# Gaps of 96 bytes between the chunks of a weight block's high and low parts

## The chip, the core and the metric

The kernel runs on one core of a Trainium2 chip. The metric is the device time of one execution in microseconds. Three timed runs of the kernel before took 2360.72, 2362.53 and 2367.87 us; the median, 2362.53, is what the change is held against.

## What is computed

Two transformer stacks, one after the other, on one sequence of 256 tokens of width 1024, all in float32. The first has two layers with three kinds of attention heads and a gated MLP; the second has two layers that mix 256 latent and 256 context tokens through a gated recurrence, a differential attention and a Fourier branch. Cut to the part that the change touches, every layer is a chain of products with large weights:

```python
for l in range(DEPTH):
    h = _rms(x, ln1[l]) * (1 + sc1) + sh1
    x = x + g1 * _mixing(h, w_in[l], ..., w_o[l], cos, sin)
    h = _rms(x, ln2[l]) * (1 + sc2) + sh2
    x = x + g2 * _swiglu(h, w_gate[l], w_up[l], w_down[l])
...
aq, ak, av, ag, ao, az, bq, bk, bv, bz, cu, cz, mg = split_cols(h @ w_in)
y = g_a * (y_a @ w_a_out) + g_b * (y_b @ w_b_out) + g_c * (y_c @ w_c_out)
return y @ w_out
```

## The kernel before

**Blocks and parts.** A weight matrix is read in blocks of up to 8 chunks; a chunk is 128 rows of the matrix, one on each partition, and mostly 256 columns. `fetch` (L356) issues the loads of a block into the tile `raw`. `split_half` (L383) then makes two tiles of it, half a block at a time: `whi`, a copy rounded to the type `float32r`, on ScalarE, and `wlo`, the rest `raw - whi`, on VectorE, or for a few blocks on POOL. There are two buffers of each, `whi0` and `whi1`, `wlo0` and `wlo1`, used in turn.

**Products.** The activations are kept as a high and a low part too: `h` (two tiles `h2`, of which the context tokens have the first half of each chunk and the latent ones the second), `ahi` and `alo` in the MLP, `part`, `fhi` and `yacc` later on. `mm3` (L505) makes a product out of three matmuls for each chunk k: high with high, high with low, low with high. All matmuls of a product add into one place in PSUM.

```python
        for k in order or range(kch):
            for i, j in ((0, 0), (0, 1), (1, 0)):
                self.nc.tensor.matmul(ps, lhsT=lsl(lhs[i], k), rhs=rsl(rhs[j], k), ...)
```

`lhsT` is the operand that is loaded into TensorE's array, 128 columns of it; `rhs` is the one that streams. Two helpers call `mm3`. In `dense_t` (L517) the weight block is loaded and the activation streams, 256 or 512 columns; a profile row shows it as `ps_..<-h,whi`. In `dense_n` (L523) the activation is loaded and the 256 columns of the block stream: `ps_mm<-whi,h`. So each product with a full block is 24 matmuls in a row, and blocks follow each other without a pause where nothing is late. The MLP and the merges at the end of a layer are made with `dense_t`, most of the projections with `dense_n`.

**Order.** The program is written out ahead of time by a planner (`Clock`, `Pipe`) that estimates when each engine is free. It reads the shapes of operands and which ranges of a tile an instruction touches.

**Places.** All tiles of a block keep their place for the whole program. A chunk of a full block takes 1024 bytes of a partition, and chunk k of `whi` or `wlo` begins k times 1024 bytes behind the tile's first byte. As the program lays its tiles out, `whi0`, `whi1`, `wlo0` and `wlo1` all begin at 160 modulo 512, and so does each of their chunks. The chunks of `h`, `part`, `fhi` and `yacc` all begin at 480 modulo 512, those of `ahi` and `alo` at 288 in the first layer and 384 in the second. One kind of block is narrow, the 16 gate columns of the second stack (`a_gates`): its chunks are 64 bytes wide and so stand at eight places modulo 512 already.

Of the kernel before, what the change touches and what calls it, by code (L numbers as in the profile page):

```python
# [8 lines left out]
F32R = mybir.dt.float32r  # L9
# [11 lines left out]
DEPTH = 2  # L21
KC = D // 128
WB = 256
D_FF = 2816
FC = D_FF // 128
EPS = 1e-6
# [277 lines left out]
class Program:  # L304
# [51 lines left out]
    def fetch(self, j, now):  # L356
        kch, pieces = self.order[j]
        if j >= 2 and j - 2 >= self.ns or (not now and self.wp.free("raw", 2) > self.clock.t["pe"] + self.p.AHD):
            return False
        t = self.wp.tile([128, KC * WB], F32, name="raw", bufs=2)  # L360
        n = sum(p[4] for p in pieces)
# [19 lines left out]
    def split_half(self, now=True):  # L381


        j = self.ns
        if j >= self.nd or (j >= 2 and j - 2 not in self.consumed):
            return False
        if not now and self.clock.ready([self.blk[j][0]]) > self.clock.t["pe"] + 1:
            return False
        raw = self.blk[j][0]
        kch, pieces = self.order[j]  # L390
        n = sum(p[4] for p in pieces)
        if self.half == 0:
            for i, nm in ((1, "whi"), (2, "wlo")):
                t = self.wp.tile([128, KC * WB], F32R, name=f"{nm}{j % 2}")
                self.blk[j][i] = t[:, :kch * n].rearrange("p (k c) -> p k c", k=kch)
        k0, k1 = ((0, (kch + 1) // 2), ((kch + 1) // 2, kch))[self.half]
        hi, lo = self.blk[j][1], self.blk[j][2]
        if k1 > k0:
            self.nc.scalar.copy(hi[:, k0:k1], raw[:, k0:k1])
            e = self.nc.gpsimd if str(self.half) in self.p.SPOOL and self.every else self.nc.vector  # L400
            e.tensor_tensor(lo[:, k0:k1], raw[:, k0:k1], hi[:, k0:k1].bitcast(F32), op=ALU.subtract)
        self.half += 1
        if self.half == 2:
            self.half = 0
            self.ns += 1
        return True
# [1667 lines left out]
```

## Time and profile before

| | |
|---|---|
| median of three runs | 2362.53 us |
| the profiled execution | 2364.57 us |
| its span, first to last instruction | 2362.8 us |
| TensorE, matmuls | 2247.8 us busy, 95% |
| TensorE, weight loads | 1974.9 us, 84% |
| VectorE | 1287.4 us, 54% |
| ScalarE | 1032.1 us, 44% |
| POOL | 371.7 us, 16% |
| mean granted clock of TensorE | 0.969 |

The busy time of an engine is the time in which at least one of its instructions runs. Matmuls are pipelined: the next begins before the last has ended, so their durations add up to more than the busy time, and the pace of a row of matmuls is read from their starts. All instructions that helpers issue have one line, L170, in this program; groups are told apart by the names of their tiles, output first, then the operands, for a matmul the streaming one before the loaded one.

### The profile page before, as it was taken

The page shows a single profiled execution, that of the slowest core. Times are in us where ns is not written, and L with a number is a line of the kernel's source. Part 1 is how long each engine was busy: PE and PEld are TensorE (multiplying, and loading weights), DVE is VectorE, ACT ScalarE, POOL GpSimd, SP SyncE. Part 2 cuts the span into 40 slices and gives each one's busy share as a digit, 9 for nine tenths or more (in the row PEclk, how much of TensorE's full clock was granted, in tenths as well). Part 3 has the DMA queues.
Part 4 walks back from the last instruction along what each step waited for, and adds up shares of the span by engine and source line. Part 5 has one row for each costly group of instructions (what it writes and reads, how often), then busy time and mean ns, then how long its engine had stood idle before and what let it go on. Part 6 is the DMA issues. An engine that isn't in the chain of part 4 may idle for free. (4 is left out here: it accounts for less than half of the span.)

```text
span 2362.8 us, 39015 instructions
## 1 busy us (share of the span) xinstructions
PE 2247.8 (95%) x15672; PEld 1974.9 (84%) x15672; DVE 1287.4 (54%) x2547; ACT 1032.1 (44%) x1994; POOL 371.7 (16%) x897
## 2 busy tenths in 40 slices
PE   7989999998899999997989999999999999989999
PEld 3756899876899988887878888888898897989999
DVE  3735556575556546666554424335364656655665
ACT  3543445445444444554543323223254445444543
POOL 3311001551000103122022000000020333220000
PEclk8978999998999999998999999999999999999999
DMA  9646985655686522122114434434343232337865
GB/s 331 230 159 220 288 252 181 212 188 196 197 243 187 173 89 72 56 82 72 61 65 139 128 91 113 119 94 114 96 131 90 81 99 74 106 114 201 211 172 170
DMA packets 395061, 348.52 MB, mean 148 GB/s; under 512 B 12768, under 2 KB 364384, under 8 KB 394368
## 3 DMA queue, kind: packets, MB, share of 16 engines
q1 hardware_dynamic: 386752, 321.29, 45.1%
q0 software_dynamic: 6688, 21.66, 2.9%
q10 hardware_dynamic: 1440, 3.08, 0.4%
q8 instruction: 123, 2.02, 0.4%
q14 instruction: 58, 0.48, 0.1%
HBM read 335.50 MB, written 10.49 MB: 146 GB/s over the span
## 5 line engine op out<-in xcount | busy, mean ns | idle before, releaser
L170 DVE TENSOR_TENSOR wlo<-raw,whi 128x1024 fp32r<-128x1024 f32 (+1 forms) x465 | 547.6, 1210 | 449.1 <-ACT whi L170 447.8
L170 ACT CAST whi<-raw 128x1024 fp32r<-128x1024 f32 (+3 forms) x476 | 471.5, 1031 | 216.1 <-PE ps_t L170 63.3
L170 PE MATMUL ps_mm<-whi,h 128*128 128x256 f32 x2752 | 533.9, 291 | 16.1 <-ACT whi L170 6.2
L170 PEld LDWEIGHTS ps_mm<-whi,h 128*128 128x128 f32 x2752 | 440.6, 194 | 48.7 <-issue 19.3
L170 PE MATMUL ps_mm<-wlo,h 128*128 128x256 f32 x1376 | 391.1, 284 | 7.5 <-DVE wlo L170 7.3
L170 PE MATMUL ps_mm<-h,whi 128*128 128x256 f32 (+2 forms) x1656 | 375.5, 321 | 1.9 <-DVE xT L170 1.8
L170 PEld LDWEIGHTS ps_mm<-h,whi 128*128 128x128 f32 (+1 forms) x1656 | 269.2, 187 | 46.9 <-issue 9.0
L170 PEld LDWEIGHTS ps_mm<-wlo,h 128*128 128x128 f32 x1376 | 266.8, 194 | 12.6 <-DVE wlo L170 8.4
L170 PE MATMUL ps_mm<-h,wlo 128*128 128x256 f32 (+2 forms) x828 | 263.0, 318 | 1.1 <-POOL wlo L170 1.1
L170 PE MATMUL ps_s<-h,whi 128*128 128x256 f32 (+1 forms) x1120 | 240.2, 310 | 0.0
L170 PE MATMUL ps_t<-h,whi 128*128 128x256 f32 (+1 forms) x1096 | 234.9, 310 | 2.1 <-ACT h L170 1.5
L170 PEld LDWEIGHTS ps_s<-h,whi 128*128 128x128 f32 x1120 | 181.3, 188 | 18.3 <-ACT th L170 5.6
L170 PEld LDWEIGHTS ps_t<-h,whi 128*128 128x128 f32 x1096 | 179.0, 190 | 19.8 <-ACT th L170 6.3
L170 PE MATMUL ps_s<-h,wlo 128*128 128x256 f32 (+1 forms) x560 | 173.4, 310 | 0.1
L170 PE MATMUL ps_t<-h,wlo 128*128 128x256 f32 (+1 forms) x548 | 169.5, 309 | 0.0
L170 PEld LDWEIGHTS ps_mm<-h,wlo 128*128 128x128 f32 (+1 forms) x828 | 155.1, 187 | 14.7 <-POOL wlo L170 1.3
L170 PE MATMUL ps_g<-gw,c 128*32 128x512 f32 (+1 forms) x640 | 100.8, 640 | 18.0 <-DMA gw<-in_w_mod_dram 8.7
L170 PEld LDWEIGHTS ps_s<-h,wlo 128*128 128x128 f32 x560 | 105.2, 188 | 7.0 <-DVE wlo L170 0.3
L170 PEld LDWEIGHTS ps_t<-h,wlo 128*128 128x128 f32 x548 | 104.2, 190 | 6.2 <-DVE wlo L170 0.2
L170 ACT ACTIVATE M<-ps_s,nmB,rsB 128x512 f32<-128x512 f32 (+1 forms) x96 | 67.0, 702 | 94.2 <-DVE nmB L170 94.2
L170 DVE SCALAR_TENSOR_TENSOR y<-th,y 128x512 f32<-128x512 f32 (+1 forms) x64 | 35.6, 556 | 81.2 <-ACT th L170 67.9
L170 POOL TENSOR_TENSOR sqa<-sqa,sq 128x256 f32<-128x256 f32 x30 | 22.1, 736 | 346.9 <-ACT sq L170 191.3
(406 smaller groups left out, 3726.8 us busy)
## 6 DMA issues: line engine op xcount, KB each, us to landing
raw<-in_w_in_dram SPq DMA_DIRECT2D x72, 1024.0 KB, 5.3
raw<-in_w_in_dram SPq DMA_DIRECT2D x100, 512.0 KB, 4.1
gw<-in_w_mod_dram SPq DMA_DIRECT2D x96, 512.0 KB, 5.3
gw<-in_w_ada_dram SPq DMA_DIRECT2D x64, 384.0 KB, 5.0
raw<-in_w_gate_dram SPq DMA_DIRECT2D x44, 512.0 KB, 4.1
raw<-in_w_up_dram SPq DMA_DIRECT2D x44, 512.0 KB, 5.6
raw<-in_w_down_dram SPq DMA_DIRECT2D x16, 1024.0 KB, 5.1
raw<-in_w_out_dram SPq DMA_DIRECT2D x12, 1024.0 KB, 5.2
```

Source lines behind the costliest of these rows:

```text
L170: return real(*a, **k)
```

## The change

A constant `WPAD` of 24 elements, 96 bytes, is added. The tiles `whi` and `wlo` become 8 times 96 bytes larger, and the view of a block in them leaves 96 bytes free behind each chunk. `raw`, the loads and the matmuls stay as they are; the copies and subtractions write (and the subtraction reads back) four rows of 256 elements with gaps instead of one row of 1024.

```diff
+WPAD = 24
...
         if self.half == 0:
             for i, nm in ((1, "whi"), (2, "wlo")):
-                t = self.wp.tile([128, KC * WB], F32R, name=f"{nm}{j % 2}")
-                self.blk[j][i] = t[:, :kch * n].rearrange("p (k c) -> p k c", k=kch)
+                t = self.wp.tile([128, KC * (WB + WPAD)], F32R, name=f"{nm}{j % 2}")
+                self.blk[j][i] = t[:, :kch * (n + WPAD)].rearrange("p (k c) -> p k c", k=kch)[:, :, :n]
```

A chunk of a full block now begins 1120 bytes behind the one before it, which is 96 modulo 512: the eight chunks of `whi` begin at 160, 256, 352, 448, 32, 128, 224 and 320 modulo 512. Each of the four tiles takes 8960 bytes instead of 8192, so that `wlo0` and `wlo1` begin at 416 modulo 512 and `whi1` at 160 as before. The order of instructions on all engines is the same, row for row; only the shapes of the copies and subtractions differ.

## Rows read from the trace of the kernel before

**Rows 1.** The page: busy time by engine, and the granted clock in 40 slices.

```profile
PE 2247.8 (95%) x15672; PEld 1974.9 (84%) x15672; DVE 1287.4 (54%) x2547; ACT 1032.1 (44%) x1994; POOL 371.7 (16%) x897
...
PEclk8978999998999999998999999999999999999999
```

**Rows 2.** Waits of PE: us in total, times, longest us.

```profile
PE ps_mm L170 <- DVE wlo L170: 7.3, 5, 2.1
PE ps_mm L170 <- ACT whi L170: 6.2, 3, 3.0
```

**Rows 3.** Groups of PE by form: xcount | busy us, mean ns | idle before.

```profile
L170 PE MATMUL ps_mm<-whi,h 128*128 128x256 f32 x2752 | 533.9, 291 | 16.1 <-ACT whi L170 6.2 <-ACT h L170 5.5 <-DVE pq L170 2.1
L170 PE MATMUL ps_mm<-wlo,h 128*128 128x256 f32 x1376 | 391.1, 284 | 7.5 <-DVE wlo L170 7.3 <-POOL wlo L170 0.2
L170 PE MATMUL ps_mm<-h,whi 128*128 128x256 f32 x1112 | 203.9, 284 | 1.9 <-DVE xT L170 1.8
L170 PE MATMUL ps_mm<-h,whi 128*128 128x512 f32 x512 | 161.6, 397 | 0.0
```

**Rows 4.** Timeline of PE, 1870.2 to 1872.9: start us, us from first start to last end.

```profile
1870.03 0.28 PE L170 MATMUL ps_mm<-wlo,h 128*128 128x256 f32 x1
...
1870.50 0.39 PE L170 MATMUL ps_mm<-whi,h 128*128 128x256 f32 x2
...
1871.18 0.39 PE L170 MATMUL ps_mm<-whi,h 128*128 128x256 f32 x2
...
1871.52 0.39 PE L170 MATMUL ps_mm<-whi,h 128*128 128x256 f32 x2
```

**Rows 5.** Timeline of PE, 1893.6 to 1896.3, first and last of an even pace.

```profile
1893.81 0.28 PE L170 MATMUL ps_mm<-wlo,h 128*128 128x256 f32 x1
...
1895.93 0.28 PE L170 MATMUL ps_mm<-wlo,h 128*128 128x256 f32 x1
```

**Rows 6.** Stretches: window, us, then busy us of each engine, PEclk, DMA share.

```profile
2141.20:2299.20 158.00, 158.00 (x1343) 157.97 (x1342) 96.78 (x136) 74.83 (x112) 4.29 (x8) 1.00 0.73 194
2300.00:2359.00 59.00, 59.00 (x523) 59.00 (x522) 36.98 (x53) 24.93 (x35) 0.00 (x0) 1.00 0.61 177
1300.00:1700.00 400.00, 400.00 (x1749) 328.19 (x1748) 160.61 (x184) 117.63 (x150) 8.59 (x16) 1.00 0.40 109
```

**Rows 7.** Timeline of PE, 1500.0 to 1501.4, 512 columns.

```profile
1500.42 0.39 PE L170 MATMUL ps_t<-part,wlo 128*128 128x512 f32 x1
1500.64 0.62 PE L170 MATMUL ps_t<-part,whi 128*128 128x512 f32 x2
```

**Rows 8.** Timeline of PE, 836.4 to 839.6, the block of 16 columns.

```profile
836.93 0.62 PE L170 MATMUL ps_mm<-h,whi 128*16 128x512 f32 x2
...
839.02 0.62 PE L170 MATMUL ps_mm<-h,whi 128*16 128x512 f32 x2
```

**Rows 9.** Timeline of PE, 404 to 405.3, the MLP's last product.

```profile
403.79 0.28 PE L170 MATMUL ps_t<-ahi,whi 128*128 128x256 f32 x1
...
405.22 0.28 PE L170 MATMUL ps_t<-ahi,whi 128*128 128x256 f32 x1
```

**Rows 10.** Timeline of PE, 1803.8 to 1805.5, 512 columns at another pace.

```profile
1804.34 0.63 PE L170 MATMUL ps_mm<-h,whi 128*128 128x512 f32 x2
...
1805.04 0.63 PE L170 MATMUL ps_mm<-h,whi 128*128 128x512 f32 x2
```

**Rows 11.** Groups of ACT and DVE by form: xcount | busy us, mean ns | idle before.

```profile
L170 ACT CAST whi<-raw 128x1024 fp32r<-128x1024 f32 x452 | 455.4, 1048 | 203.0 <-PE ps_mm L170 60.0 <-PE ps_t L170 57.5 <-PE ps_s L170 53.0
...
L170 ACT CAST whi<-raw 128x768 fp32r<-128x768 f32 x16 | 12.5, 832 | 13.1 <-PE ps_t L170 5.8 <-PE ps_s L170 4.9 <-PE ps_mm L170 2.4
...
L170 ACT ACTIVATE eB<-eB 128x768 f32<-128x768 f32 x8 | 6.5, 841 | 0.2
...
L170 DVE TENSOR_TENSOR wlo<-raw,whi 128x1024 fp32r<-128x1024 f32 x441 | 529.0, 1232 | 426.2 <-ACT whi L170 425.0 <-PE ps_mm L170 0.5
...
L170 DVE TENSOR_TENSOR oB<-oB,roB 128x1024 f32<-128x1024 f32 x4 | 4.9, 1223 | 6.0 <-POOL roB L170 6.0
```

## The prediction

> **What bounds the kernel now.** I read the page's busy shares first [rows 1]: TensorE is busy for 2247.8 of 2362.8 us (95%), and the granted clock is nine tenths or more in nearly every slice; VectorE stands at 54%, ScalarE at 44%. Next come the waits of TensorE [rows 2]: the longest entry on a weight block is 7.3 us for `wlo` and 6.2 us for `whi`, eight waits in all. So the splits that the change reshapes are hidden, and what counts is how fast one matmul follows another.
>
> Then the groups by form give the numbers of matmuls [rows 3]. The change touches the two operands of every one that reads a weight block: 4,128 that stream 256 columns of `whi` or `wlo` (2752 + 1376), about 6,400 that stream 256 columns of an activation over weights loaded from `whi` or `wlo`, and about 2,250 of the second kind with 512 columns. That is nearly all of TensorE's time.
>
> The pace is read from starts in the timeline, since durations overlap. The reader should see that identical matmuls with 256 columns run at two paces. In [rows 4] a group of 24 begins unevenly (from 1870.03 to 1870.50 are four, 118 ns each) and then settles at 0.34 us for three, 113.3 ns each. In [rows 5] a group of the same form stays at 117.8 ns: from 1893.81 to 1895.93 are eighteen, in 2.12 us. Long stretches say the same [rows 6]: 158.0 us hold 1343 matmuls, the next 59.0 us 523. One or two of each count reach over the edges, which makes 117.8 and 113.3 ns, for the same kind of matmul at the same granted clock of 1.00, the 2.4 GHz level. With 512 columns 400.0 us hold 1749 (229 ns). A pace, once found, is kept: nothing in the other engines' columns goes with it.
>
> Counted over all starts inside unbroken runs of equal matmuls (the first and last of them being rows like those), the mean is 115.4 ns where the weight block streams (3,632 intervals, about half at each pace), 117.05 where it is loaded (5,907, mostly the slow pace) and 229.1 with 512 columns (2,213).
>
> **What the change does to this.** Before, each of a block's chunks begins at 160 modulo 512 and each chunk of `h` at 480, so that every matmul of a run meets its weight load in the same relation, and a steady pace can form. Afterwards the relation moves by 96 bytes at every chunk, that is every three matmuls, and `wlo` starts 256 away from `whi` besides. My reading is that no pace can settle, and that TensorE works on as it does where it has not settled.
>
> The trace has that state. At the start of runs the first three intervals have a mean of 117.3 ns where the block streams (134 runs), 117.4 where it is loaded (65 runs) and 231.7 with 512 columns (23 runs), before the settled means above. Two other rows agree. The block of 16 columns already stands at eight places modulo 512, its chunks being 64 bytes apart: from 836.93 to 839.02 nine matmuls take 232.2 ns each [rows 8]. And where `ahi` and `alo` stream, at 288 modulo 512 instead of 480, twelve take 119.2 ns each, from 403.79 to 405.22, and keep neither pace [rows 9]. Against it: the 16 columns are a short load, and `ahi` keeps one relation throughout, so neither is the changed state itself.
>
> **The sum**, against the profiled execution's 2364.57 us (span 2362.8):
> - block streams: 3,632 x (117.3 - 115.4) = +6.9 us;
> - block is loaded, 256 columns: 5,907 x (117.4 - 117.05) = +2.1 us;
> - 512 columns: 2,213 x (231.7 - 229.1) = +5.8 us.
>
> That is +14.8 us of TensorE, of which 95% (its busy share) reaches the end: +14.1. The matmuls outside unbroken runs are set by what they wait for and are taken at nothing. 2364.57 is 2.0 above the median of the three runs, so 2362.5 + 14.1 gives 2376.6, in round numbers **2377 us**.
>
> The cost of an unsettled pace lies between bounds. Below: every run finds the fast pace, 113.3 ns, and the 512-column ones the 226 ns that is the shortest of the three intervals that repeat there (1500.42 to 1500.64 in [rows 7]; the other two are 229 and 232). That is 3,632 x 2.1 + 5,907 x 3.75 + 2,213 x 3.1 = 36.6 us, down to 2326. Above: 118.8 ns, the mean with `ahi` and `alo` over 296 intervals, and 233.3, at which one group with 512 columns already stands: from 1804.34 to 1805.04 are three [rows 10]. That is 12.3 + 10.3 + 9.3 = 32 us, up to 2394. I take the start-of-run value, which is nearest to a relation that keeps changing, and keep both ends for the range.
>
> **The other edits.** The casts and subtractions write four rows of 256 with a gap instead of 1024 in one piece. ScalarE shows rows with a gap: `eB`, two rows of 384, takes 841 ns where the flat cast of 768 takes 832 [rows 11], so 9 ns for one gap and some 27 for three; I allow twice that, 54. 452 casts give 24 us of ScalarE's time at the most, under TensorE's. VectorE's `oB`, also in rows, takes 1223 ns for 1024 where the flat subtraction takes 1232: nothing. POOL, busy for 16% [rows 1], does 11 of the subtractions; no row of it has gaps at that size, and if they took half as long again, the block that they belong to would still be needed later. If the cover fails, the eight waits for a block grow by 0.05 us each: 0.4 us. A split that got faster would gain no more than those waits, 13.5 us. The low and high tiles grow by 768 bytes each; what stands after them moves by 3072 bytes, six times 512, so nothing else changes place modulo 512. The order of all instructions, DMAs and loads is the same row for row; no queue is passed and no wait added.
>
> **A rule against this.** The rows show paces that differ by 4.5 ns with nothing else changed. The Trainium skill, TensorE: Matmul & The Clock Gate, section Step-by-step: what each phase is for, says that TensorE reads the streamed operand and the weights through two independent ports, so that a load takes nothing from the running matmul; its section Back-to-back issue gap puts the gap at N / 2.4 + 2.5 ns, an estimate of 109.2 and 215.8 ns here. The trace disagrees with the figures: no settled pace is below 113.3 and 229. By that rule the places don't matter and the time stays at 2362.5.
>
> **The rivals.**
> 1. *It makes no difference* (0.19). What sets the pace is the rhythm of starts, not bytes. For it: two paces at equal addresses [rows 6], and the 16-column block, whose intervals don't follow its moving place [rows 8]. Against it: the pace with `ahi` is neither of the two [rows 9]. Then the gaps alone are left and hidden: 2362.5, within 3 us. That the change doesn't take effect at all belongs here; the tiles are laid out anew for every block, so I don't expect it.
> 2. *It is faster* (0.25). The mechanism: loads and streams that begin at the same place hold each other up at each start, and this is the slow pace; at eight places most chunks miss each other, and a run that misses once falls into 113.3 and stays, as in [rows 4]. The place is the loaded blocks, 5,907 intervals now mostly at 117.8. It decides the sign when three in ten runs come to the fast pace: 0.3 x 36.6 us is then as much as 0.7 x 14.8. All of them give 2326, half of the saving 2344. Against it: the fast pace also needs a steady relation, as far as any row shows.
> 3. *It is slower by more* (in my 0.56): every chunk meets a relation like that of [rows 9], 2394.
>
> **How the numbers follow.** About 0.3% (7 us) is what a measurement of this kernel can tell from no change. The forecast case has 0.56; some 0.05 of it ends below 2369.6 and counts as the same. With rival 1 that makes 0.24 the same; rival 2 is faster, 0.25; slower is left with 0.51. The range reaches to 2396 for rival 3 and down to 2336, seven tenths of rival 2's saving, and leaves out the ends of both. The forecast case alone runs from 2364 to 2396.
>
> **What would show it.** In the changed profile: if right, the timeline of a group of 24 has no settled 0.34 or 0.35 us for three, 158 us of the last stretch hold about 1,340 matmuls again, the stretch of 59 us fewer than 523, and 400 us of 512-column work about 1,727 instead of 1,749. Right for the splits: `whi` up to 1.10 us, waits of TensorE for blocks near 13 us. If the last stretch moves to 1,390 or more in 158 us, rival 2 holds; if both paces are found again with sharp steps between runs, rival 1. I would be wrong in the size if the unsettled mean is not 117 but near one of the ends, and in the mechanism if a pace settles in spite of the moving places.

## The result and the profile after

The changed kernel takes 2377.66 us (median of five runs, 2374.23 to 2382.75) where the kernel before takes 2360.72 (five runs, 2353.09 to 2367.87): a ratio of 1.0072, with a 95% interval of 1.0051 to 1.0094. That is 17 us slower. The profiled execution after is the one of 2377.66 us, its span 2375.9, its mean granted clock 0.978 (before 0.969).

The page's busy line and granted clock answer to [rows 1]:

```profile
PE 2256.8 (95%) x15672; PEld 1978.3 (83%) x15672; DVE 1289.5 (54%) x2547; ACT 1031.0 (43%) x1994; POOL 371.4 (16%) x897
...
PEclk9988999999999999998999999999999999999999
```

The other engines have not moved by more than 2.1 us; TensorE is busy for 9.0 us more. The splits with gaps, and the waits of PE for them, answer to [rows 11] and [rows 2]:

```profile
L171 DVE TENSOR_TENSOR wlo<-raw,whi 128x1024 fp32r<-128x1024 f32 x441 | 531.7, 1238 | 434.0 <-ACT whi L171 432.5 <-PE ps_mm L171 0.7
L171 ACT CAST whi<-raw 128x1024 fp32r<-128x1024 f32 x452 | 454.9, 1047 | 207.9 <-PE ps_mm L171 61.4 <-PE ps_t L171 60.1 <-PE ps_s L171 54.1
```

```profile
PE ps_mm L171 <- DVE wlo L171: 6.5, 5, 1.8
PE ps_mm L171 <- ACT whi L171: 6.1, 3, 3.0
```

Three gaps in an instruction cost nothing: 1047 ns against 1048, 1238 against 1232, and the eight waits come to 12.6 us against 13.5. So the loss lies in the matmuls. By form they answer to [rows 3], all four a little longer:

```profile
L171 PE MATMUL ps_mm<-whi,h 128*128 128x256 f32 x2752 | 540.0, 292 | 16.6 <-ACT whi L171 6.1 <-ACT h L171 5.3 <-DVE pq L171 2.1
L171 PE MATMUL ps_mm<-wlo,h 128*128 128x256 f32 x1376 | 391.6, 285 | 6.6 <-DVE wlo L171 6.5
...
L171 PE MATMUL ps_mm<-h,whi 128*128 128x256 f32 x1112 | 205.9, 286 | 1.8 <-DVE xT L171 1.8
...
L171 PE MATMUL ps_mm<-h,whi 128*128 128x512 f32 x512 | 163.3, 400 | 0.0
```

And the stretches of [rows 6], in which TensorE is busy throughout at a granted clock of 1.00:

```profile
1300.00:1700.00 400.00, 400.00 (x1720) 322.44 (x1719) 158.14 (x181) 116.51 (x148) 9.13 (x17) 1.00 0.39 106
2141.20:2299.20 158.00, 158.00 (x1337) 157.91 (x1336) 96.68 (x135) 74.31 (x110) 6.44 (x12) 1.00 0.73 196
2300.00:2359.00 59.00, 59.00 (x499) 58.84 (x498) 40.45 (x60) 28.88 (x43) 0.00 (x0) 1.00 0.69 195
```

400 us hold 1720 matmuls of 512 columns, not 1749; the last two stretches run at nearly the same pace now, 158.0 us over 1337 and 59.0 over 499 (118.2 ns each), where one of them had 113.3. The stretch of 158 us had the slower pace before too, so its 1337 against 1343 says little; the stretch of 59 us and the streaming groups tell. The group of [rows 4], which settled at 0.34 us for three matmuls, now reads in the timeline of PE:

```profile
1879.83 0.40 PE L171 MATMUL ps_mm<-whi,h 128*128 128x256 f32 x2
...
1880.53 0.39 PE L171 MATMUL ps_mm<-whi,h 128*128 128x256 f32 x2
...
1880.87 0.40 PE L171 MATMUL ps_mm<-whi,h 128*128 128x256 f32 x2
...
1881.23 0.40 PE L171 MATMUL ps_mm<-whi,h 128*128 128x256 f32 x2
...
1881.94 0.28 PE L171 MATMUL ps_mm<-whi,h 128*128 128x256 f32 x1
```

From the first to the last are 18 matmuls in 2.11 us, 117.2 ns each; three take 0.34 us once and 0.36 the next time. Single intervals of the group lie between 113 and 123 ns, and none repeats as a rhythm.

Counted much as the prediction counts (3,632, 5,907 and 2,213 intervals there), over all starts inside unbroken runs of equal matmuls at full clock, in the two profiled executions (the loaded blocks parted by what streams):

| class | intervals before | before, ns | after, ns | more, us |
|---|---|---|---|---|
| block streams, 256 columns | 3,679 | 115.4 | 118.3 | 10.6 |
| block loaded, `h` streams, 256 | 3,961 | 117.0 | 118.3 | 5.2 |
| block loaded, `part`, `fhi`, `yacc`, 256 | 1,144 | 116.4 | 118.4 | 2.3 |
| block loaded, `ahi`, `alo`, 256 | 1,051 | 118.5 | 118.3 | -0.2 |
| block loaded, 512 columns | 2,213 | 229.1 | 232.7 | 8.1 |

That is 26.0 us more, of which the medians show 17 and this pair 13.1. Part of the difference is the clock. Around 175 us the profile of before has a long stretch at the lower level, of which that of after has little; the window from 160 to 190 us, of before and of after (the granted clock, 0.66 and 0.94, stands third from the end):

```profile
160.00:190.00 30.00, 24.63 (x116) 13.83 (x116) 12.71 (x53) 11.08 (x36) 0.00 (x0) 0.66 0.50 161
```

```profile
160.00:190.00 30.00, 24.08 (x164) 14.07 (x164) 16.41 (x71) 13.59 (x48) 0.00 (x0) 0.94 0.60 196
```

In all, TensorE stood at the 1.2 GHz level for 147.0 us before and for 106.3 after. At half the pace 40.7 us would be worth some 20 us of work at the most. Two estimates from the runs are lower: over the 66 executions of the kernel before in the comparisons below a mean clock higher by 0.001 goes with a time shorter by some 1.2 us, which makes 11 us of this pair's 0.009; and over the thirteen profiled executions each us less at the lower level goes with a span some 0.4 us shorter than the counted paces alone would make it, which makes 16. With 11 to 16 us taken off, 26.0 is near the 13.1 us of this pair. It need not be the change's doing: those 66 executions have mean clocks from 0.968 to 0.978, so that this pair can have happened to get one from either end.

### The profile page after: what moved, and what is told of

Read it like the earlier page. It is cut to its first block, busy times and chain, and to the rows that moved or that the text cites. A ratio compares the mean times of both kernels' runs of the same rounds, so it can differ in the third digit from the quotient of the medians.

```text
span 2375.9 us, 39015 instructions
## 1 busy us (share of the span) xinstructions
PE 2256.8 (95%) x15672; PEld 1978.3 (83%) x15672; DVE 1289.5 (54%) x2547; ACT 1031.0 (43%) x1994; POOL 371.4 (16%) x897
## 5 line engine op out<-in xcount | busy, mean ns | idle before, releaser
L171 PE MATMUL ps_mm<-whi,h 128*128 128x256 f32 x2752 | 540.0, 292 | 16.6 <-ACT whi L171 6.1
L171 PE MATMUL ps_g<-gw,c 128*32 128x512 f32 (+1 forms) x640 | 96.0, 618 | 19.8 <-DMA gw<-in_w_mod_dram 10.1
```

The lines of the kernel that those rows point to most:

```text
L171: return real(*a, **k)
```

## The experiments

All twelve differ from the kernel before in places alone. "Intervals" are counted as in the table above. Ratios stand with their 95% intervals, against the kernel before in the same comparison. Call **d** the place of the loaded operand less the place of the streaming one, modulo 256, at the load that runs beside the stream. Before, d is 192 where a block is loaded past `h` (160 less 480), and 64 where the block streams past a loaded `h`.

**e1: the same gaps in `h` too**, so that block and `h` chunks keep their relation while both change places.

```diff
-                t = self.wp.tile([128, KC * WB], F32R, name=f"{nm}{j % 2}")
-                self.blk[j][i] = t[:, :kch * n].rearrange("p (k c) -> p k c", k=kch)
+                t = self.wp.tile([128, KC * (WB + 24) + 64], F32R, name=f"{nm}{j % 2}")
+                self.blk[j][i] = t[:, :kch * (n + 24)].rearrange("p (k c) -> p k c", k=kch)[:, :, :n]
...
-        self.h2 = [p2.tile([128, KC, T2], F32R, name=f"h2{i}") for i in range(2)]
+        self.h2 = [p2.tile([128, KC * (T2 + 24) + 64], F32R, name=f"h2{i}")[:, :KC * (T2 + 24)].rearrange(
+            "p (k c) -> p k c", k=KC)[:, :, :T2] for i in range(2)]
```

> The weight blocks have the gaps of 96 bytes, and the chunks of h get the same gaps, so that a chunk of the block and the chunk of h that it meets keep one relation modulo 512, while both stand at eight places. Theory (a pace settles where the relation is the same at every chunk): the products with h come back to even paces, means near 115.4 ns where the block streams, 117 where it is loaded, 229 with 512 columns; only the products with part, fhi, yacc, ahi and alo stay near 118.3 and 232.7. Time 1.000 to 1.003 of the kernel before. Rival 1 (eight places are themselves the cost, whatever the other operand does): 118.3 and 232.7 everywhere, 1.007.

Measured: 2381.25 us against 2358.96, 1.0086 (1.0059 to 1.0113). Streams 117.5 ns, loads with `h` 118.3, 512 columns 232.9. The paces of before did not come back, which at first I took to mean that the relation doesn't matter and a moving place does. Parted by d the same intervals say something else: the 2,513 stream intervals inside a chunk (d = 64) have a mean of 115.2 ns, as before, and the 1,186 at a chunk's border, where the next chunk is loaded beside the last stream of this one (d = 64 + 96 = 160), take 122.3. Equal gaps keep the relation within a chunk and not across its border. The loads with `h` don't part in this way: within a chunk, where d is 192 as before, they take 118.7 ns instead of 117.0, and at the border (d = 32) 117.6. So in a kernel whose d changes, the pace of an interval doesn't hang on its own d alone.

**e2: only `wlo` displaced by 256 bytes**, as the change does besides its gaps.

```diff
+                t = self.wp.tile([128, KC * WB + 128], F32R, name=f"{nm}{j % 2}")
+                d = 64 * (i == 2)
+                self.blk[j][i] = t[:, d:d + kch * n].rearrange("p (k c) -> p k c", k=kch)
```

> No gaps; only wlo0 and wlo1 begin 256 bytes later, at 416 modulo 512, as they do in the change. Theory: the relation is still the same at every chunk, so runs settle, each at one even pace or a repeating one; time 0.995 to 1.005. Rival 2 (the distance of whi and wlo is the cost, not the gaps): intervals as in the change, 118.3 ns and 232.7, time 1.007.

Measured: 2356.74, 0.9992 (0.9973 to 1.0011); streams 115.4, loads with `h` 117.2, 512 columns 229.1. The displacement of `wlo` is not the cause.

**e3: gaps of 64 bytes** instead of 96 (`WPAD` = 16).

> Gaps of 64 bytes instead of 96: eight places modulo 512 again, but every chunk keeps its place modulo 64, and wlo begins where whi does. Theory: the relation changes at every chunk, so no pace settles: 117.5 to 119 ns, 231 to 233, time 1.005 to 1.009. Rival 3 (what costs is that every second chunk changes its place within 64 bytes): paces and time as before, 1.000.

Measured: 2376.29, 1.0064 (1.0040 to 1.0087); 117.9, 118.1 and 231.7. A place that stays constant modulo 64 helps little.

**e4: no gaps, all blocks displaced by 256 bytes** (to 416 modulo 512).

```diff
+                t = self.wp.tile([128, KC * WB + 128], F32R, name=f"{nm}{j % 2}")
+                self.blk[j][i] = t[:, 64:64 + kch * n].rearrange("p (k c) -> p k c", k=kch)
```

> No gaps; whi and wlo both begin 256 bytes later, at 416 modulo 512, one relation for all chunks, but another one. Theory: runs settle; which pace they find is open, 113.3 to 120 ns, so the time lies anywhere from 0.985 to 1.01. Rival 4 (the relation of before is a good one by luck, and any other costs as much as the change): uneven intervals with a mean of 118 ns or more, 1.007 or slower.

Measured: 2355.45, 0.9991 (0.9972 to 1.0011); 115.1, 117.0 and 229.1; only the small class of loads with `part`, `fhi` and `yacc` moved, from 116.4 to 117.8. The place modulo 512 isn't what counts; modulo 256 nothing had changed.

**e5: gaps in `h` alone** (the second half of e1's edit), blocks as before.

> Here the chunks of h get the gaps of 96 bytes (places 480, 64, 160, ... modulo 512) and the weight blocks none (160 throughout). Theory now held, after the run with equal gaps in both (a constant relation, and still 1.0086): what costs is that an operand's place changes from chunk to chunk, whichever operand it is. Then the products of a weight block with h run at about 118 ns (256 columns) and 232.5 ns (512 columns), while the loaded blocks with part or ahi/alo, where nothing changes, keep their 116.4 to 117.8 and 118.5 ns and 228.9 ns with 512; the time is 1.006 to 1.008 of before. Rival: only the places of W count (its tiles are new for every block): then all paces are those of before and the time is 0.998 to 1.002. The relation theory would also give unsettled paces here, but it has already failed with the equal gaps.

Measured: 2377.16 against 2362.86, 1.0048 (1.0029 to 1.0067), a little under what was expected. Streams 118.4, loads with `h` 118.2, 512 columns with `h` 231.3, and where `part` streams, which has no gaps, 115.2 and 229.4. It costs whichever operand moves, and only in the products where one does.

**e6: gaps only in blocks that stream.**

```diff
+                name, c = pieces[0][0], pieces[0][3]
+                streams = name == "w_in" and c not in (QB, QB + 256) or name == "w_in_2" and (
+                    AV <= c < AG or BQ <= c < BZ or CU <= c < CZ)
+                g = 24 if streams else 0
+                self.blk[j][i] = t[:, :kch * (n + g)].rearrange("p (k c) -> p k c", k=kch)[:, :, :n]
```

> Only the weight blocks that stream past h get the gaps of 96 bytes; blocks that are loaded into TensorE keep 160 for whi, and 416 for wlo (a displacement by 256 alone had cost nothing). Theory held: the cost is additive by class, so streams go from 115.4 to about 118.2 ns (3,700 intervals, +10.5 us) while loaded blocks stay at 117 ns and 512 columns at 229.1; time 1.003 to 1.006 of before. Rival: an unsettled stretch leaves its rhythm to the next runs, so that the others become slower too (512 columns above 231): 1.007 or more. Rival: the streams' term is given back elsewhere (waits, clock): within 1.002.

Measured: 2366.35, 1.0010 (0.9997 to 1.0023), below the 1.003 expected. The streams' term came as expected, 118.2 ns, +10.4 us. But loads with `h`, whose blocks had got no gaps (their `wlo` alone stood 256 bytes further on, as in e2), ran at 115.9 instead of 117.0 (-4.3 us) and with `part` at 115.0 (-1.6). The last stretch shows it, 1383 matmuls where [rows 6] has 1343:

```profile
2141.20:2299.20 158.00, 157.52 (x1383) 156.94 (x1382) 100.28 (x139) 77.97 (x117) 4.83 (x9) 1.00 0.73 199
```

At one and the same d both paces of before occur, 113.3 and 117.8. Which of them a stretch has may hang on what ran before it, since that is what this edit changed; it is not shown, as one execution of each kernel was profiled.

**e7: gaps of 256 bytes in `whi`**, so that d modulo 256 stays as it was though places change at every chunk.

```diff
+                e = 64 if i == 1 else 0
+                t = self.wp.tile([128, KC * (WB + e)], F32R, name=f"{nm}{j % 2}")
+                self.blk[j][i] = t[:, :kch * (n + e)].rearrange("p (k c) -> p k c", k=kch)[:, :, :n]
```

> Gaps of 256 bytes in whi alone, so that its chunks stand at 160 and 416 modulo 512 by turns; wlo and h as before. By the theory that only places modulo 256 count (a displacement of everything by 256 had left each class of paces within 0.4 ns, 1.0 ns for one), the paces stay 115.4, 117 and 229.1 and the time is 0.998 to 1.002 of before: a gap and a change of place by itself cost nothing. By the rival that any change of place from chunk to chunk keeps a pace from settling, two matmuls in three are unsettled, streams run at about 118, loaded blocks at 118, 512 columns at 231 to 232.7, and the time is 1.005 to 1.008.

Measured: 2360.86, 0.9990 (0.9980 to 1.0001); 115.3, 117.2 and 229.1. Neither a gap nor a change of place costs anything as long as d stays.

**e8: no gaps, all blocks displaced by 64 bytes**, so that d is 0 in every product with `h` and `part` and never changes (e4's edit with 16 elements in the place of 64).

> No gaps; all blocks stand at 224 modulo 512 instead of 160, so that block and h (480) agree modulo 256. If the value of a constant place matters as little as a shift by 256 did, paces and time are those of before, 0.998 to 1.002. If the constant relation sets which pace a run finds (the runs with ahi and alo, in another relation, have a steady 118.5 ns), the classes move together: to 113.3 ns and 226 to 229 ns (0.985 to 0.995 of before) where this relation is a good one, or to 118.5 and about 233 (1.006 to 1.009) where it is a bad one.

Measured: 2382.64, 1.0079 (1.0055 to 1.0104). A constant place, and slower than the changed kernel's gaps at 256 columns: loads with `h` 119.9, streams 119.7, most intervals 120; while 512 columns got faster, to 227.1. The paces of the two kinds move apart, which neither alternative had. In the windows, 1319 matmuls in 158 us and 1766 in 400 us:

```profile
1300.00:1700.00 400.00, 400.00 (x1766) 331.24 (x1765) 163.52 (x188) 119.96 (x153) 9.66 (x18) 1.00 0.40 110
2141.20:2299.20 158.00, 158.00 (x1319) 158.00 (x1319) 94.62 (x132) 74.22 (x110) 6.10 (x12) 1.00 0.71 195
```

The timeline of PE in a streaming group of e8 is perfectly even, 18 matmuls in 2.16 us:

```profile
1897.75 0.40 PE L170 MATMUL ps_mm<-whi,h 128*128 128x256 f32 x2
...
1898.11 0.40 PE L170 MATMUL ps_mm<-whi,h 128*128 128x256 f32 x2
...
1899.91 0.28 PE L170 MATMUL ps_mm<-whi,h 128*128 128x256 f32 x1
```

**e9, e10, e11: three more constant displacements**, by 128, 192 and 224 bytes (32, 48 and 56 elements). In loads with `h` d is 64, 128 and 160, in streams 192, 128 and 96.

> No gaps; all blocks at 288 modulo 512, so that a loaded block stands 64 above h modulo 256 and h stands 192 above a block that streams (before: 192 and 64; with the shift by 64: 0 and 0). Theory now held: each constant distance modulo 256 between load and stream has a pace of its own, and gaps only lead a kernel through several of them, so that it gets their mean. The gaps of 64 bytes walk through exactly the four distances 0, 64, 128 and 192, with 118.06 ns (loaded, h), 117.85 (stream) and 231.7 (512). With what is known of two distances (116.95 and 119.9; 115.4 and 119.7; 229.1 and 227.0) the two that are left, this run and the next, should have means of 117.7 (loaded), 118.1 (stream) and 235 ns (512) between them; for this one alone I expect about 116.4 loaded and 116.6 stream (the values at these distances in the changed kernel), time 0.998 to 1.005 of before. Rival: any constant distance but 0 settles near the paces of before (115.4, 117, 229) in both runs, and a moving place costs something by itself: both within 1.002.

> No gaps; all blocks at 352 modulo 512: the distance is 128 modulo 256 both ways. By the theory of one pace for each distance: about 117.9 ns loaded (the value at this distance in the changed kernel) to 119, 118.7 stream, 232 to 236 with 512 columns, time 1.006 to 1.012 of before; together with the run before it the means 117.7, 118.1 and 235. By the rival (a moving place costs by itself): 115.4, 117 and 229, within 1.002.

> No gaps; all blocks at 384 modulo 512: loaded blocks stand 160 above h, h stands 96 above a streaming block. In the changed kernel this was the slowest distance for loads (120.8 ns) and a slow one for streams (118.9), 233.2 with 512 columns. By the theory of one pace for each distance: loads above 119.5 ns, streams above 118, 512 columns 232 or more; time 1.009 to 1.016 of before, the slowest of all runs so far without any gap. By the rival (only moving places or equal places cost): within 1.002.

Measured against 2359.82: e9 2360.99, 1.0005 (0.9989 to 1.0021); e10 2382.56, 1.0098 (1.0071 to 1.0125); e11 2391.95, 1.0136 (1.0106 to 1.0166). Loads with `h`, streams, 512 columns: e9 113.7, 117.4 and 233.3; e10 119.0, 118.7 and 232.4; e11 119.9, 118.1 and 233.3. The rival, that a constant place is harmless unless it is an equal one, falls: the slowest of all thirteen kernels has no gap. For e9 I had expected 116.4 for loads; nearly all of them found 113.3 (13 us less, and 2.5 with `part`), and 512 columns (9 us more) and streams (7 us more) gave it back. The windows of e9:

```profile
1300.00:1700.00 400.00, 400.00 (x1716) 322.28 (x1715) 156.92 (x180) 115.41 (x146) 8.58 (x16) 1.00 0.38 105
2141.20:2299.20 158.00, 157.18 (x1379) 156.58 (x1379) 100.30 (x139) 77.91 (x117) 4.83 (x9) 1.00 0.74 200
```

of e10:

```profile
2141.20:2299.20 158.00, 158.00 (x1320) 158.00 (x1319) 94.84 (x132) 74.22 (x110) 6.07 (x12) 1.00 0.72 195
```

and of e11:

```profile
1300.00:1700.00 400.00, 400.00 (x1716) 321.82 (x1715) 159.09 (x182) 117.16 (x150) 10.19 (x19) 1.00 0.40 107
2141.20:2299.20 158.00, 158.00 (x1319) 158.00 (x1318) 95.00 (x132) 74.31 (x110) 8.04 (x15) 1.00 0.72 194
```

The last stretch is loaded blocks with 256 columns: 1343 matmuls in 158 us at d = 192 [rows 6], 1319 at 0, 1379 at 64, 1320 at 128, 1319 at 160. The timeline of PE of e9 keeps 0.34 us for three from block to block, here 30 matmuls in 3.40 us:

```profile
2200.10 0.39 PE L170 MATMUL ps_s<-h,whi 128*128 128x256 f32 x2
...
2200.44 0.39 PE L170 MATMUL ps_s<-h,whi 128*128 128x256 f32 x2
...
2203.50 0.39 PE L170 MATMUL ps_mm<-h,whi 128*128 128x256 f32 x2
```

With these runs the pace at each constant d can be set out (`ahi` and `alo` stand at a different constant d in each kernel, and give the rest):

| d | 256 columns, ns | 512 columns, ns |
|---|---|---|
| 0 | 119.9 loads, 119.7 streams (e8), 120.0 `ahi` (e9) | 227.1 |
| 32 | 118.3 `ahi` (before) | |
| 64 | 113.7 loads (e9), 115.4 streams (before), 115.9 `ahi` (e10) | 233.3 |
| 96 | 118.1 streams (e11), 117.4 `ahi` (e11) | |
| 128 | 119.0 loads, 118.7 streams (e10), 118.7 `ahi` (before) | 232.4 |
| 160 | 119.9 loads (e11), 120.0 `ahi` (e9) | 233.3 |
| 192 | 117.0 loads (before), 117.4 streams (e9), 117.8 `ahi` (e8) | 229.1 |
| 224 | 116.7 `ahi` (e10) | |

It makes little difference which operand is the weight: the same d gives the same pace within 0.3 ns at 0 and 128, within 0.8 at 96 and 192, and within 2.2 at 64, where two paces are open. A pace at a constant d need not be even: in the last stretch nearly all intervals of e8 are 120 ns and those of e9 113 or 114, but e10 goes in turns through 117 or 118, 120, and 122 or 123.

**e12: each kind at a d of its own choice.** Blocks that are loaded for 512 columns stand at 224 modulo 512 (d = 0), all others as before.

```diff
+                t = self.wp.tile([128, KC * WB + 128], F32R, name=f"{nm}{j % 2}")
+                name, l, _, c = pieces[0][:4]
+                streams = AV <= c < AG or BQ <= c < BZ or CU <= c < CZ
+                s = 16 if name == "w_in_2" and l == 0 and not streams else 0
+                self.blk[j][i] = t[:, s:s + kch * n].rearrange("p (k c) -> p k c", k=kch)
```

> No gaps; the blocks that are loaded for 512 columns stand at 224 modulo 512 as in the shift by 64 (226.7 to 227.2 ns there, 229 before), all the others at 160 as before. By the theory the paces of the classes keep apart: 512 columns 227.0 ns (2,200 intervals, 4.7 us less), 115.4 and 117 as before: 0.998 of before, 0.997 to 0.9995. Rival: a run takes its pace over from the run ahead of it, so that 512 columns stay at 229 or the others rise: 1.000 or above.

Measured: 2353.29 against 2359.82, 0.9970 (0.9954 to 0.9987). It is faster than both kernels. 512 columns took 227.1 ns; the other classes stayed at 115.2 and 117.2. Its windows have 1775 matmuls in the 400 us in which [rows 6] has 1749, and the pace of before in the last stretch. Of the 1775 the last 19 have 256 columns, since the faster kernel has left its 512-column work by then; e8's 1766 is the count of the 512-column pace itself.

```profile
1300.00:1700.00 400.00, 400.00 (x1775) 331.61 (x1774) 159.75 (x183) 116.64 (x149) 7.52 (x14) 1.00 0.39 107
2141.20:2299.20 158.00, 157.91 (x1341) 157.70 (x1340) 100.08 (x144) 75.99 (x115) 4.29 (x8) 1.00 0.71 193
```

Moving the blocks that are loaded for 256 columns to d = 64 as well would, by e9's 113.7 ns over 3,961 intervals and 114.2 over 1,144, save another 15 us or so (an estimate from those rows). This was not tried.

## Why the prediction was right, and where it was not

**The time and the sign.** Forecast 2377, measured 2377.66. The forecast of a slower kernel through the pace of matmuls, with splits and waits unchanged, is what the profile shows: `whi` 1047 ns (up to 1.10 us was allowed), waits 12.6 us (near 13), 1337 matmuls in the stretch of 158 us (about 1,340, but 1343 before), 499 in that of 59 us (fewer than 523), 1720 in 400 us (about 1,727).

**The sum's terms** were too small. Unsettled paces of 117.3, 117.4 and 231.7 were taken from the first three intervals of runs; the changed kernel has 118.3, 118.3 and 232.7. Term by term: streams +10.6 for +6.9, loaded blocks +7.3 for +2.1, 512 columns +8.1 for +5.8, in all 26.0 for 14.8. The start of a run is a short state at the old d and no proxy for a stretch at other ones.

**The share that reaches the end** was taken as 95%. Of the 26.0 us the medians show 17. Over the thirteen kernels the counted sum is above the difference that the ratio gives each time, by 1.4 to 9.0 us and by 4.5 in the mean, whether the sum is large or small. That looks like an offset rather than a share; what makes it stays open. For the changed kernel the 9.0 is the largest of all. Its five executions have granted clocks of 0.973 to 0.978, median 0.976, those of before in the later comparisons a median of 0.973; at some 1.2 us for 0.001, as above, 0.003 would be some 4 us. That is an estimate, and five executions don't settle it. So the number was met by luck: a sum too small by 11 us met a share too large by some 8 (95% of 26.0 would be 24.7, not 17) and a base, 2362.53, that lies 1.8 above the median of five.

**The mechanism** was right in that no pace settles in the changed kernel. It failed at the next step, that settling is what is lost, so that the start of a run prices the loss. What counts is the distance d modulo 256 between load and stream. A constant distance settles in a rhythm of its own, and that may be a slower one than the changed kernel's mean of 118.3 (loads with `h`: 119.9 in e8, 119.0 in e10, 119.9 in e11); a moving place that keeps d costs nothing (e7). The gaps of 96 bytes lead each product through all eight multiples of 32, and the pace comes out near their mean: the rows of the table for 256 columns have a mean of 118.0 ns (of the values in a row the mean is taken first), against 118.3 measured; the five known for 512 columns have 231.0 against 232.7. By those means streams lose 9.6 of their 10.6 us, loaded blocks 5.3 of 7.3, and 512 columns 4.2 of 8.1: three quarters of the 26. e3 is the cleaner case, since gaps of 64 bytes visit just the four distances 0, 64, 128 and 192: their constant paces have means of 117.8 (streams), 117.4 (loads with `h`) and 230.5 (512 columns), and e3 has 117.9, 118.1 and 231.7. The rest, 0.1 to 1.2 ns there, may be what moving through them costs besides. This is an agreement of means, and not of single intervals. Parted by d, the changed kernel's loads with `h` do have 120.8 ns at 160 and 116.5 at 64; but its 512 columns with `h` take 232.2 at d = 0, where a constant 0 has 227.1, and in e3 loads with `h` and streams lie between 117.5 and 118.6 at every d, where constant ones have 113.7 to 119.9. That the loss comes from the changing distances is shown; that each distance adds its own pace to it is not.

**The rivals.** Rival 1, no difference because places don't matter, is out. The Trainium skill, TensorE: Matmul & The Clock Gate, section Step-by-step: what each phase is for, has it that a weight load takes no read bandwidth from the running matmul; the trace disagrees as far as the start places go, since a displacement of all blocks by 64 bytes alone moved loads from 117.0 to 119.9 ns (e8). The formula that the prediction took from the section Back-to-back issue gap of the same page of the Trainium skill stands there for the isolated gap of a single matmul, so that 109.2 and 215.8 ns are no forecast for a row of loads and matmuls; no settled pace here lies below 113.3 and 226.7. Rival 2 said that loads and streams at the same place hold each other up. At d = 0 that is so for 256 columns, but for 512 columns d = 0 is the best distance found. Its fast pace did come, in e9 by a constant distance and not by moving places. Rival 3, slower by more, was nearer for the paces (118.8 and 233.3 against 118.3 and 232.7) than the forecast, but not for the time. One more rival, which the prediction doesn't name, is that the writes of ScalarE and VectorE into the displaced tiles meet TensorE's reads. It doesn't fit e8: in the stretch of 158 us shown above 1,259 of 1,285 intervals are 120 ns, although VectorE works in only 94.62 us of it.

**What stays open:** what in the memory makes a distance good or bad, why 256 and 512 columns prefer different ones, and what chooses between the two paces at d = 64 and 192.

## What to carry to other kernels

Where TensorE is the bound and matmuls follow each other without a pause, look at the byte places of the loaded and the streaming operand: here their distance modulo 256 was worth up to 6 ns in 120 per matmul, and the kernel's time went from 0.997 to 1.014 of before by nothing else. Read the pace from counts in busy windows, and try a few constant displacements for each shape apart, as the best distance for one shape was a bad one for another. Padding between chunks is not neutral: it costs the copies nothing, but it trades the distance one has for something near a mean over several, unless the pad keeps it (256 bytes did).

## What was not expected of the hardware

- The same matmul at the same clock takes 113.7 to 119.9 ns with 256 columns and 227.1 to 233.3 with 512, by the distance of its operands' places modulo 256, all else equal (e8 to e11). At distances of 64 and 192 two paces are open.
- Moving the blocks by 256 bytes, or their two parts against each other by 256, leaves streams, loads with `h` and 512 columns within 0.3 ns of before (e2, e4, e7); loads with `part`, `fhi` and `yacc` vary by 1.4 ns.
- A class of products whose places modulo 256 were untouched ran at 115.9 instead of 117.0 ns when other products changed their pace (e6): at a distance with two paces, what ran before may decide, which is not shown.
